# Expert stage: spill and read-back transfers of late chunks issued by ACT, transposes two steps later, three weight loads in flight

## The chip, the cores and the metric

One core of a Trainium2 chip runs the whole program in one launch. The metric is the device time of that launch in microseconds (us). The kernel before has three timed runs with a median of 2337.91 us (2332.89 to 2342.59); one further execution was profiled. The engines are named as in the profile: PE multiplies matrices (PEld is its loading of the stationary operand), DVE and ACT work on vectors, POOL issues indirect DMAs, SP issues the plain loads.

## What is computed

Two transformer blocks on 512 tokens of width 1024, all in float32. The change touches only the last stage, the mixture of experts of the second block. Each token goes to 4 of 32 experts, and each expert is a clamped SwiGLU with its own weights:

```
logits = xt @ router_w + router_b
top_val, top_idx = lax.top_k(logits, TOP_K)          # 4 of 32
gate = softmax(top_val)
# for the tokens of expert e:
gu = xblk @ w_gu[e] + b_gu[e]                         # 1024 -> 2048
g, up = gu[:, :1024], gu[:, 1024:]
g = minimum(g, 7.0); up = clip(up, -7.0, 7.0)
act = (up + 1.0) * (g * sigmoid(1.702 * g))
y = act @ w_down[e] + b_down[e]                       # 1024 -> 1024
out[token] += gate * y
```

An expert's weights are 8 MiB for `w_gu` and 4 MiB for `w_down`. All 32 experts' weights are read once, 384 MiB in all, and the routing decides at run time how many tokens each expert has: 64 on average (512 x 4 / 32).

## The kernel before

Before the experts come the first block, the mixer of the second block and the routing; the experts run from about 984 us of the span to its end, and the last few tens of microseconds add the result to the residual.

**Weights.** `Moe.load` (lines 1625 to 1640) issues one DMA of 1 MiB for each weight tile, on SP's queue: eight `gu` tiles and four `dn` tiles per expert, in the order gu(0), gu(1), dn(0), gu(2), dn(1) and so on. The tiles lie in a ring of 21 slots (`RING = 5, 16`), and a load needs a free slot. `turn` (line 1642) adds a second condition: with `FLIGHT = 2`, a load waits until the load two places before it has landed. Only the first five loads, issued ahead of the stage by `ahead`, are free of it.

**Tokens.** The tokens of an expert are cut in chunks of 64. Chunk 0 is always computed, chunk 1 in two quarter passes of 32 tokens if the expert has over 64 (and over 96) tokens, and each later chunk c if there are over 64c. These are nested `tc.If` blocks on the register `r`. `fetch` gathers a chunk's rows with an indirect DMA on POOL's queue, four transposes on PE bring it into the layout of the stationary operand (`transposed`, tile `ptx`, read out by DVE into `xT` or `turned`), and `up` multiplies with the `gu` tiles and applies the SwiGLU. `down` transposes the activations likewise (read out by ACT), multiplies with the `dn` tiles, scales by the gate on ACT (tile `y`, line 1621) and adds the result to `acc` in DRAM with an indirect DMA on POOL's queue (line 1623).

**Order.** `run` calls, for each e, `tile_up(e)`, the loads that refill the slots it has used, the gathers for later experts, `tile_down(e - 1)` and again the loads that refill its slots. Each queue runs its instructions in order.

**Late chunks.** The activations of chunk 0 and 1 stay on the chip. Those of chunk 2 and later are too many for that: `tile_up` writes the tile `late` (128 x 512, 256 KB) to the DRAM array `spill` (line 1709), and `tile_down` reads it back (lines 1732 and 1747). Both transfers are on POOL's queue. In `down`, `mid` places the four transposes of the next chunk inside the loop over k of 0 to 7, behind the matmuls of k = 4; the last quarter pass, `down(4, e, 1, ...)`, transposes `late` for chunk 2 there.

Of the kernel before, what the change touches and what calls it, by code (L numbers as in the profile page):

```python
# [64 lines left out]
def sm_tile(g, name):  # L65
    return g.ps.tile([P, 512], F32, tag="sm", bufs=2, name=name)


def uid(g, s):
    g.n += 1  # L70
    return f"{s}_{g.n}"
# [47 lines left out]
def behind(g, after, before):  # L119

    g.tc.add_manual_dep(after.ins, before.name, mybir.DependencyInfo(mybir.DependencyClass.NoSync, mybir.DependencyReason.DATA), reason="in turn")
# [1195 lines left out]
NCH = T // CH  # L1317
QUARTERS = 2
RING = 5, 16
FLIGHT = 2  # L1320
LATE = 9
PACE = 2
FILLS = 8
# [3 lines left out]
class Moe:  # L1327
# [265 lines left out]
                mid()  # L1593
        self.swiglu(act, pg, pu, N)

    def down(self, n, e, c, aT, mid=None, after=None):

        g = self.g
        nc = g.nc
        W = self.W["dn", e]  # L1600
        w, N = P // n, D // n
        nb = N // P
        py = sm_tile(g, uid(g, "py"))[:, :N]
        if n == 2:
            d = nc.tensor.matmul(py, self.sel[e], self.bias[:, 2, :], start=True, stop=False)
        else:
            aT = aT[:, c * nb:(c + 1) * nb]
            for odd in range(2):
                x = nc.tensor.matmul(py, self.quarters(e, odd), self.bias[:, 2, odd * N:(odd + 1) * N], start=not odd, stop=False)
                d = d if odd else x  # L1610
        if after is not None:
            behind(g, d, after)
        for k in range(KD):
            lhs = aT[:, k % nb, (k // nb) * w:(k // nb + 1) * w]
            for h in range(n):
                o = (k % 2) * D + h * N
                nc.tensor.matmul(py[h * w:(h + 1) * w, :], lhs, W[k // 2][:, o:o + N], start=False, stop=(k == KD - 1))  # L1617
            if k == 4 and mid is not None:
                mid()
        y = self.pool.tile([P, 512], F32, tag="y", bufs=2, name=uid(g, "y"))[:, :N]  # L1620
        nc.scalar.mul(y, py, self.gate[n][:, c, e:e + 1])
        acc = self.acc if n == 2 else self.acc.rearrange("r (h n) -> (r h) n", h=2)
        nc.gpsimd.indirect_dma_start(out=acc, out_offset=bass.IndirectOffsetOnAxis(ap=self.idx[n][:, c, e:e + 1], axis=0), in_=y, in_offset=None, compute_op=ALU.add)  # L1623
# [18 lines left out]
    def turn(self, d, limit=True):  # L1642

        if limit and len(self.flight) >= FLIGHT:
            self.g.tc.add_manual_dep(d, self.flight[-FLIGHT], mybir.DependencyInfo(mybir.DependencyClass.Sync, mybir.DependencyReason.SCHED_ONLY), reason="few loads at a time")
        self.flight.append(d.name)
# [45 lines left out]
    def tile_up(self, e, xT):  # L1692

        g, tc, r, x = self.g, self.g.tc, self.r[e], self.late
        act0, act1 = self.pool.tile([P, 512], F32, tag="act0", bufs=1, name=uid(g, "act")), self.act1[e % 2]
        more = self.hinted(e, CH, "up")
        self.up(2, e, xT, act0, mid=lambda: self.transposed(self.x1, self.turned(1)))

        def chunk(c, more):
            with tc.If(r > c * CH, label=more):
                then = None
                if c + 1 < NCH:
                    more = self.hinted(e, (c + 1) * CH, "up")
                    self.fetch(x[(c + 1) % 2], e, c + 1)
                    then = lambda: self.transposed(x[(c + 1) % 2], self.turned(c + 1))
                self.up(2, e, self.turned(c), x[c % 2], mid=then, at=6)
                g.nc.gpsimd.dma_start(self.spill[e % 2, c - 2], x[c % 2])
                if c + 1 < NCH:  # L1710
                    chunk(c + 1, more)

        with tc.If(r > CH, label=more):
            with tc.If(r > 2 * CH):
                self.fetch(x[0], e, 2)
            more = self.hinted(e, CH + CH // 2, "up")
            self.up(4, e, self.turned(1), act1[:, 0:256], 0)
            with tc.If(r > CH + CH // 2, label=more):
                more = self.hinted(e, 2 * CH, "up")
                self.up(4, e, self.turned(1), act1[:, 256:512], 1, mid=lambda: self.transposed(x[0], self.turned(2)))  # L1720
                chunk(2, more)
        return act0, act1

    def tile_down(self, e, aT, act1, more, after):
        g, tc, r, a = self.g, self.g.tc, self.r[e], self.late
        self.down(2, e, 0, aT, mid=lambda: self.transposed(act1, self.turned(1), 0.5), after=after)

        def back(c):

            if c < NCH:  # L1730
                with tc.If(r > c * CH):
                    g.nc.gpsimd.dma_start(a[c % 2], self.spill[e % 2, c - 2])

        def chunk(c, more):
            with tc.If(r > c * CH, label=more):  # L1735
                back(c + 2)
                then = None
                if c + 1 < NCH:
                    more = self.hinted(e, (c + 1) * CH, "down")
                    then = lambda: self.transposed(a[(c + 1) % 2], self.turned(c + 1), 0.5)  # L1740
                self.down(2, e, c, self.turned(c), mid=then)
                if c + 1 < NCH:
                    chunk(c + 1, more)

        with tc.If(r > CH, label=more):  # L1745
            with tc.If(r > 2 * CH):
                g.nc.gpsimd.dma_start(a[0], self.spill[e % 2, 0])
                back(3)
            more = self.hinted(e, CH + CH // 2, "down")
            self.down(4, e, 0, self.turned(1))  # L1750
            with tc.If(r > CH + CH // 2, label=more):
                more = self.hinted(e, 2 * CH, "down")
                self.down(4, e, 1, self.turned(1), mid=lambda: self.transposed(a[0], self.turned(2), 0.5))
                chunk(2, more)

    def turned(self, c):
# [191 lines left out]
```

## Time and profile before

| | us |
|---|---|
| median of three runs | 2337.91 |
| range of the runs | 2332.89 to 2342.59 |
| the profiled execution, whole | 2348.3 |
| its span, first to last instruction | 2346.5 |
| PE busy in the span | 2046.9 (87%) |

The profile is of one execution. Its span is 1.8 us shorter than its time, and its time is 10.4 us above the median of the runs. The share of a DMA engine's time that packets took and the rate in GB/s are means over 16 engines. PEclk is TensorE's granted clock as a share of 2.4 GHz, so 0.50 is 1.2 GHz. A row of waits reads: engine and tile, the releaser, us in total, how often, the longest.

### The profile page before, as it was taken

What the parts mean: (1) busy time and instruction counts of PE and PEld (TensorE: products, weight loads), DVE (VectorE), ACT (ScalarE), POOL (GpSimd) and SP (SyncE); (2) the same over time, 40 slices, a digit from 0 to 9 for tenths busy, and PEclk for the clock granted to TensorE, in tenths of its full rate; (3) what the DMA queues carried; (4) which work ended last, traced back from release to release, by engine and by line L of the source; (5) the groups of instructions that cost most, each with busy time, mean ns of one, the idle gap of its engine ahead of it and who ended that gap; (6) DMA issues with size and microseconds to landing.
All of it is one profiled execution on the core that took longest, in us unless ns stands there. A gap on an engine that the chain in (4) does not pass through costs nothing. (4 is left out here: it accounts for less than half of the span.)

```text
span 2346.5 us, 31249 instructions
## 1 busy us (share of the span) xinstructions
PE 2046.9 (87%) x11586; PEld 1116.4 (48%) x11589; DVE 860.5 (37%) x1891; ACT 476.4 (20%) x839; POOL 333.1 (14%) x329
## 2 busy tenths in 40 slices
PE   6999988999998999789898997766798899898763
PEld 6856765688877977533333332221233333333211
DVE  6466659764556556522121121111121122121112
ACT  3345332234434124200100100000000110000001
POOL 2000226310013221100101101000001110101002
PEclk9999999999999999789999999999999999999997
DMA  6451476852237625898939899999996799999986
GB/s 194 119 169 52 154 195 187 252 175 92 98 104 213 213 75 196 345 337 292 327 143 323 300 337 331 356 329 337 325 356 231 257 329 330 336 349 342 333 323 204
DMA packets 213970, 584.24 MB, mean 249 GB/s; under 512 B 32287, under 2 KB 107438, under 8 KB 179822
## 3 DMA queue, kind: packets, MB, share of 16 engines
q1 hardware_dynamic: 182688, 523.74, 62.3%
q0 software_dynamic: 16784, 46.94, 7.4%
q10 hardware_dynamic: 14142, 9.10, 1.3%
q8 instruction: 189, 3.10, 0.5%
q14 instruction: 167, 1.37, 0.2%
HBM read 537.88 MB, written 41.84 MB: 247 GB/s over the span
## 5 line engine op out<-in xcount | busy, mean ns | idle before, releaser
L1587 PE MATMUL pg<-wgu,xT 128*64 128x512 f32 x1024 | 281.5, 620 | 77.9 <-DMA wgu<-in_exp_w_gu 72.5
L1587 PE MATMUL pu<-wgu,xT 128*64 128x512 f32 x1024 | 272.5, 603 | 3.5 <-issue 3.5
L1617 PE MATMUL py<-wdn,aT 128*64 128x512 f32 x1024 | 241.7, 604 | 34.0 <-DMA wdn<-in_exp_w_down 33.9
L1547 DVE TENSOR_TENSOR turned<-ptx,cols 128x512 f32<-128x512 f32 x42 | 29.1, 692 | 461.7 <-PE ptx L1539 460.4
L1561 ACT ACTIVATE th<-gm 128x512 f32<-128x512 f32 (+1 forms) x54 | 30.2, 560 | 777.4 <-DVE gm L1560 762.9
L89 DVE TENSOR_TENSOR wlo<-wst,whi 128x1024 fp32r<-128x1024 f32 (+1 forms) x109 | 135.4, 1242 | 126.6 <-ACT whi L88 126.5
L88 ACT CAST whi<-wst 128x1024 fp32r<-128x1024 f32 (+2 forms) x121 | 123.9, 1027 | 257.7 <-DMA wst<-in_w_ff_in 82.5
L1587 PEld LDWEIGHTS pg<-wgu,xT 128*64 128x64 f32 x1024 | 66.7, 139 | 228.5 <-DMA wgu<-in_exp_w_gu 124.5
L1587 PEld LDWEIGHTS pu<-wgu,xT 128*64 128x64 f32 x1024 | 76.6, 140 | 155.1 <-issue 155.1
L1623 POOL DMA_INDIRECT acc<-y,idx x54 | 85.7, 1587 | 445.5 <-ACTq L1745 226.0
L1617 PEld LDWEIGHTS py<-wdn,aT 128*64 128x64 f32 x1024 | 66.2, 136 | 166.4 <-issue 105.8
L1657 DVE CAST sel<-pick 128x128 fp32r<-128x128 f32 x32 | 7.7, 239 | 357.5 <-PEq L1735 151.1
L1591 PE MATMUL pgu<-wgu,turned 128*32 128x512 f32 x1152 | 128.6, 594 | 0.0
L98 PE MATMUL pf<-hTh,whi 128*128 128x512 f32 (+1 forms) x288 | 111.2, 390 | 8.6 <-ACT whi L88 6.2
L100 PE MATMUL pf<-hTh,wlo 128*128 128x512 f32 (+1 forms) x288 | 109.5, 383 | 6.9 <-DVE wlo L89 6.9
L99 PE MATMUL pf<-hTl,whi 128*128 128x512 f32 (+1 forms) x288 | 109.5, 381 | 0.0
L1531 POOL DMA_INDIRECT xg<-hn,idx x32 | 33.1, 1033 | 491.8 <-PE ptx L1539 415.5
L1617 PE MATMUL py<-wdn,turned 128*32 128x256 f32 (+1 forms) x1280 | 101.2, 418 | 0.0
L98 PE MATMUL plt<-whi,ahi 128*128 128x512 f32 x256 | 99.6, 389 | 0.0
L99 PE MATMUL plt<-wlo,ahi 128*128 128x512 f32 x256 | 99.6, 389 | 0.0
L100 PE MATMUL plt<-whi,alo 128*128 128x512 f32 x256 | 99.1, 389 | 0.0
L1560 DVE TENSOR_SCALAR gm<-pg 128x512 f32<-128x512 f32 x36 | 24.9, 691 | 155.0 <-PE pg L1587 150.4
(541 smaller groups left out, 3423.8 us busy)
## 6 DMA issues: line engine op xcount, KB each, us to landing
wgu<-in_exp_w_gu SPq DMA_DIRECT2D x256, 1024.0 KB
wdn<-in_exp_w_down SPq DMA_DIRECT2D x128, 1024.0 KB
wst<-in_w_in SPq DMA_DIRECT2D x36, 512.0 KB
wst<-in_w_ff_in SPq DMA_DIRECT2D x32, 512.0 KB
wst<-in_w_ff_out SPq DMA_DIRECT2D x32, 512.0 KB
ada_w<-in_ada_w SPq DMA_DIRECT2D x24, 512.0 KB
a<-in_ada_w SPq DMA_DIRECT2D x24, 512.0 KB
wst<-in_w_out SPq DMA_DIRECT2D x16, 512.0 KB
```

Source lines behind the costliest of these rows:

```text
L88: g.nc.scalar.copy(hi, st)
L89: eng.tensor_tensor(out=lo, in0=st, in1=hi.bitcast(F32), op=ALU.subtract)
L98: g.nc.tensor.matmul(out, ah, bh, start=start, stop=False)
L99: g.nc.tensor.matmul(out, ah, bl, start=False, stop=False)
L100: g.nc.tensor.matmul(out, al, bh, start=False, stop=stop)
L1531: self.g.nc.gpsimd.indirect_dma_start(out=x, out_offset=None, in_=self.hn, in_offset=bass.IndirectOffsetOnAxis(ap=self.idx[2][:, c, e:e + ...
L1547: g.nc.vector.tensor_tensor(out=out, in0=src, in1=col(1), op=ALU.mult)
L1561: nc.scalar.activation(th, gm, AF.Tanh, scale=0.851)
L1587: nc.tensor.matmul(ps[h * w:(h + 1) * w, :], lhs, W[k][:, o + h * N:o + (h + 1) * N], start=False, stop=(k == KD - 1))
L1591: nc.tensor.matmul(both[h * w:(h + 1) * w], lhs, wk[:, h], start=False, stop=(k == KD - 1))
L1617: nc.tensor.matmul(py[h * w:(h + 1) * w, :], lhs, W[k // 2][:, o:o + N], start=False, stop=(k == KD - 1))
L1623: nc.gpsimd.indirect_dma_start(out=acc, out_offset=bass.IndirectOffsetOnAxis(ap=self.idx[n][:, c, e:e + 1], axis=0), in_=y, in_offset=None ...
```

## The change

The transfers of late chunks, out to `spill` and back, are issued by ACT (`nc.scalar`) in place of POOL (`nc.gpsimd`). `down` gets an argument `at`, and the calls for quarter pass 1 and for late chunks place the transposes behind k = 6 in place of k = 4; chunk 0 and quarter pass 0 are left as they were. `FLIGHT` is 3: a load waits for the load three places before it.

```diff
--- before.py
+++ after.py
@@ -1317,7 +1317,7 @@
 NCH = T // CH
 QUARTERS = 2
 RING = 5, 16
-FLIGHT = 2
+FLIGHT = 3
 LATE = 9
 PACE = 2
 FILLS = 8
@@ -1593,7 +1593,7 @@
                 mid()
         self.swiglu(act, pg, pu, N)
 
-    def down(self, n, e, c, aT, mid=None, after=None):
+    def down(self, n, e, c, aT, mid=None, after=None, at=4):
 
         g = self.g
         nc = g.nc
@@ -1615,7 +1615,7 @@
             for h in range(n):
                 o = (k % 2) * D + h * N
                 nc.tensor.matmul(py[h * w:(h + 1) * w, :], lhs, W[k // 2][:, o:o + N], start=False, stop=(k == KD - 1))
-            if k == 4 and mid is not None:
+            if k == at and mid is not None:
                 mid()
         y = self.pool.tile([P, 512], F32, tag="y", bufs=2, name=uid(g, "y"))[:, :N]
         nc.scalar.mul(y, py, self.gate[n][:, c, e:e + 1])
@@ -1706,7 +1706,7 @@
                     self.fetch(x[(c + 1) % 2], e, c + 1)
                     then = lambda: self.transposed(x[(c + 1) % 2], self.turned(c + 1))
                 self.up(2, e, self.turned(c), x[c % 2], mid=then, at=6)
-                g.nc.gpsimd.dma_start(self.spill[e % 2, c - 2], x[c % 2])
+                g.nc.scalar.dma_start(self.spill[e % 2, c - 2], x[c % 2])
                 if c + 1 < NCH:
                     chunk(c + 1, more)
 
@@ -1729,7 +1729,7 @@
 
             if c < NCH:
                 with tc.If(r > c * CH):
-                    g.nc.gpsimd.dma_start(a[c % 2], self.spill[e % 2, c - 2])
+                    g.nc.scalar.dma_start(a[c % 2], self.spill[e % 2, c - 2])
 
         def chunk(c, more):
             with tc.If(r > c * CH, label=more):
@@ -1738,19 +1738,19 @@
                 if c + 1 < NCH:
                     more = self.hinted(e, (c + 1) * CH, "down")
                     then = lambda: self.transposed(a[(c + 1) % 2], self.turned(c + 1), 0.5)
-                self.down(2, e, c, self.turned(c), mid=then)
+                self.down(2, e, c, self.turned(c), mid=then, at=6)
                 if c + 1 < NCH:
                     chunk(c + 1, more)
 
         with tc.If(r > CH, label=more):
             with tc.If(r > 2 * CH):
-                g.nc.gpsimd.dma_start(a[0], self.spill[e % 2, 0])
+                g.nc.scalar.dma_start(a[0], self.spill[e % 2, 0])
                 back(3)
             more = self.hinted(e, CH + CH // 2, "down")
             self.down(4, e, 0, self.turned(1))
             with tc.If(r > CH + CH // 2, label=more):
                 more = self.hinted(e, 2 * CH, "down")
-                self.down(4, e, 1, self.turned(1), mid=lambda: self.transposed(a[0], self.turned(2), 0.5))
+                self.down(4, e, 1, self.turned(1), mid=lambda: self.transposed(a[0], self.turned(2), 0.5), at=6)
                 chunk(2, more)
 
     def turned(self, c):
```

## Rows read from the trace of the kernel before

**Rows 1.** The page, busy time: engine, us, share, instructions.
```profile
PE 2046.9 (87%) x11586; PEld 1116.4 (48%) x11589; DVE 860.5 (37%) x1891; ACT 476.4 (20%) x839; POOL 333.1 (14%) x329
```

**Rows 2.** Windows: stretch, length, busy PE/PEld/DVE/ACT/POOL, PEclk, DMA share, GB/s.
```profile
1335.00:1658.00 323.00, 246.15 (x1166) 79.45 (x1163) 54.75 (x94) 23.51 (x38) 27.23 (x21) 0.98 0.93 337
1880.00:2150.00 270.00, 254.88 (x1626) 94.12 (x1624) 55.18 (x102) 26.02 (x45) 33.57 (x25) 0.99 0.95 342
2150.00:2302.00 152.00, 112.08 (x517) 34.41 (x515) 23.35 (x40) 11.07 (x18) 9.37 (x7) 0.98 0.91 328
```

**Rows 3.** Waits of PE from 1335 to 1724 us.
```profile
PE pg L1587 <- DMA wgu<-in_exp_w_gu: 46.5, 35, 4.7
PE py L1617 <- DMA wdn<-in_exp_w_down: 24.5, 20, 2.3
```

**Rows 4.** Waits of PE from 2150 to 2310 us.
```profile
PE pg L1587 <- DMA wgu<-in_exp_w_gu: 26.0, 22, 3.7
PE py L1617 <- DMA wdn<-in_exp_w_down: 9.5, 8, 1.9
```

**Rows 5.** Waits of PE over the expert stage, 984 to 2320 us, transposes alone.
```profile
PE ptx L1539 <- DMA late<-spill: 14.2, 2, 7.5
...
PE ptx L1539 <- issue: 5.3, 1, 5.3
```

**Rows 6.** Waits of SP's queue from 1335 to 1658 us, longest group.
```profile
SPq L1635 <- DMA wgu<-in_exp_w_gu: 139.6, 49, 6.2
```

**Rows 7.** Waits of SP's queue from 1880 to 2302 us, the one for PE.
```profile
SPq L1638 <- PEq L1718: 12.4, 1, 12.4
```

**Rows 8.** DMA view, 1335 to 1658 us: queues (packets, MB, share) and issues.
```profile
q1 hardware_dynamic: 18168, 102.54, 85.2%
q0 software_dynamic: 2320, 5.38, 6.9%
...
wgu<-in_exp_w_gu SPq DMA_DIRECT2D x66, 1024.0 KB
wdn<-in_exp_w_down SPq DMA_DIRECT2D x32, 1024.0 KB
```

**Rows 9.** Timeline of SP's queue, 914 to 919 us: start, us, line, issues.
```profile
914.51 3.48 SPq L1635 DMA_DIRECT2D wgu<-in_exp_w_gu  x5
```

**Rows 10.** Windows, columns as in Rows 2, two more stretches.
```profile
919.00:929.00 10.00, 10.00 (x58) 8.02 (x57) 4.98 (x13) 4.06 (x12) 1.30 (x1) 1.00 0.99 415
1100.00:1150.00 50.00, 44.51 (x333) 16.73 (x329) 7.57 (x15) 4.48 (x8) 6.82 (x5) 0.97 0.99 357
```

**Rows 11.** Timeline, first expert with late chunks, back transfer: start, us, instruction, [idle before].
```profile
1272.09 0.69 ACT L1621 ACTIVATE y<-py,gate 128x512 f32<-128x512 f32 x1 [2.19 <-PE py L1617]
...
1274.04 1.26 POOL L1732 DMA_DIRECT2D late<-spill  x1
...
1276.38 2.37 PE L1617 MATMUL py<-wdn,turned 128*32 128x256 f32 x40
...
1285.45 1.09 PE L1539 MATMUL ptx<-ident,late 128*128 128x128 f32 x4 [6.70 <-DMA late<-spill]
1286.47 2.79 PE L1617 MATMUL py<-wdn,turned 128*32 128x256 f32 x24
```

**Rows 12.** Windows, columns as in Rows 2, just behind that wait.
```profile
1286.00:1290.00 4.00, 4.00 (x30) 1.51 (x30) 0.00 (x0) 1.07 (x2) 0.00 (x0) 0.50 0.94 294
```

**Rows 13.** Timeline, second and third expert with a late chunk.
```profile
1779.90 0.69 ACT L1621 ACTIVATE y<-py,gate 128x512 f32<-128x512 f32 x1 [2.19 <-PE py L1617]
...
1784.69 0.61 POOL L1747 DMA_DIRECT2D late<-spill  x1
...
1832.44 0.69 ACT L1621 ACTIVATE y<-py,gate 128x512 f32<-128x512 f32 x1 [2.19 <-PE py L1617]
...
1835.84 0.60 POOL L1747 DMA_DIRECT2D late<-spill  x1 [0.82 <-DMA xg<-hn,idx]
```

**Rows 14.** DMA view of the whole span, issues of POOL: count, KB, median us to landing.
```profile
spill<-late POOLq DMA_DIRECT2D x4, 256.0 KB, 6.2
late<-spill POOLq DMA_DIRECT2D x4, 256.0 KB, 9.3
...
acc<-y,idx POOLq DMA_INDIRECT x54, 7.6
```

## The prediction, made before the change was run

> **What bounds the kernel now.** I read the page first: PE is busy 87% of the span [rows 1], so a gain must come from the places where PE waits. The waits of PE name two causes that this change touches. The first is weights. From 1335 to 1724 us PE waits 46.5 + 24.5 = 71.0 us for `wgu` and `wdn` tiles [rows 3], and from 2150 to 2310 us another 26.0 + 9.5 = 35.5 us [rows 4]. The windows agree: PE is busy 246 of 323 us in the first stretch and 112 of 152 us at the end, while the DMA engines are at 0.93 and 0.91; between them, from 1880 to 2150 us, PE is busy 255 of 270 us and is the bound itself [rows 2]. The second cause is the read-back of late activations: 14.2 us in two waits, and a third of 5.3 us that the profile files under "issue" [rows 5] and that is the same place in the third expert with a late chunk. In SP's own waits the loads of the first stretch wait for earlier loads, not for PE: the largest group alone is 139.6 us [rows 6]. So a load there is held back by the limit of two in flight, and not by a full ring. From 1880 us on only one wait for PE remains, at the beginning [rows 7].
>
> **Three in flight.** In the first stretch 66 + 32 = 98 loads are issued in 323 us [rows 8], 3.30 us each. How short could that be? Nothing in the trace shows three in flight, so I bound it from both sides.
> The far bound is the five loads that are issued without a limit in 3.48 us [rows 9]: while they land the engines are at 0.99 and move 415 GB/s [rows 10]. 1 MiB at 415 GB/s takes 1.049/0.415 = 2.53 us. POOL's traffic takes 6.9% of the engines in the first stretch [rows 8], 0.069 x 323 / 98 = 0.23 us per load, and stays. That is 2.76 us, or 0.54 us saved per load.
> The near bound is the idle share alone: the engines idle 7% [rows 2], and if packets keep their present length a full queue gives 3.30 x 0.93 = 3.07 us, 0.23 us saved. Packets are longer now than in the stretch of five loads: weights take 0.852 x 323 / 98 = 2.81 us of engine time per load against 0.99 x 2.53 = 2.50. If that is restarting after gaps, it goes too; if it is interference, it stays.
> Below both lies nothing: if one of the 16 engines is always the last, a load more in flight only lets the other 15 wait longer. A loss per load is excluded as far as I see, since the queue works its loads in the order in which they were issued.
> I take 3.00 us, 0.30 saved, near the bound of the idle share, since three is nearer to two than to five.
> First stretch: 98 x 0.30 = 29 us, under the 71.0 that PE waits. The first expert's loads start from a full ring and can't be early, so I count 25 (19 for 0.23, 46 for 0.54).
> Last stretch: loads that come earlier between 1880 and 2150 us fill the ring while PE is the bound and shorten nothing at once. What counts is the loads of the five experts that are computed at the end, 60 x 0.30 = 18 us, under the cap of 35.5 (14 for 0.23, 32 for 0.54).
>
> **Read-back by ACT, transposes at k = 6.** In the first expert with late chunks ACT's `y` ends at 1272.09 + 0.69 = 1272.78. POOL issues its scatter first and the read-back at 1274.04; PE reaches the transposes at 1276.38 + 2.37 = 1278.75 and starts them at 1285.45, 6.70 us late [rows 11]. ACT has no scatter ahead of it. I give it 0.4 us for the branch, so 0.8 us are won in the issue. In the second and third expert ACT's `y` ends at 1780.59 and 1833.13, POOL's issue is at 1784.69 and 1835.84 [rows 13], so 3.7 and 2.3 us are won. `at=6` puts 16 more matmuls ahead of the transposes, 16 x 2.37/40 = 0.95 us of work per wait.
> How long the transfer takes on ACT's queue no row shows. On POOL's queue the read-back lands after 9.3 us in the median, and the write-out, as large but mostly with no scatter queued just ahead, after 6.2 [rows 14]. With the latency unchanged 0.8 + 3.7 + 2.3 + 3 x 0.95 = 9.7 us of the 19.5 go. With 6.2 us the first lands at 1279.4, when PE has work until 1279.7, and nearly all go.
> The waits have a second price. Behind the first one the four transposes take 1.09 us and 24 matmuls 2.79 us, where 40 took 2.37 [rows 11], so 24 should take 1.42; the granted clock there is 0.50, the level of 1.2 GHz, and PE was idle just before [rows 12]. That is 1.4 us on the matmuls and some 0.5 on the transposes, 1.9 per wait, 5.7 for three, and it goes if the wait gets short. So this part is worth 9.7 to 25 us. I take 21, near the upper end, because the row of the write-out is the nearer one: it too is a plain transfer with nothing of its own queue ahead.
> All of it is on the path: in those experts PE, not the loads, is late, and the loads behind them wait for its slots, up to the last wait for PE at 1880 us [rows 7].
> A page speaks against it. The Trainium skill's page "DMA: Bandwidth & Descriptors", section "Issuing engines are not separate DMA queues", says that DMAs of all issuing engines run on the same 16 engines and interleave, so that another issuer only saves the time to start them. By that this part gives the lower end, 9.7 us.
> The rest costs about nothing. The write-out is behind ACT's tanh and has to wait for DVE's last operations, but the next ACT instruction of that block waits for PE anyway, and it happens four times [rows 14]. POOL loses eight issues. Later transposes leave eight matmuls of cover for ACT's read-out, 0.5 us against the 0.69 of an ACT operation on such a tile [rows 11]: at most 0.2 us in some ten passes, cover being the next pass's bias matmuls.
>
> **Sum.** 25 + 18 + 21 = 64 us. The profiled execution took 2348.3 us, so it would take 2284.3; it stood 10.4 us above the median of the runs, 2337.9, which gives 2274.
>
> **The rivals.**
> (a) Packets were long only because of restarts, and three in flight act like five: 46 + 32 + 21 = 99, 2239 us. For it: 415 GB/s at 0.99 [rows 10]. Against it: POOL had nothing to move then.
> (b) There is a ceiling below that. In the expert stage the best stretch of 50 us that I found moved 357 GB/s at 0.99 of the engines [rows 10]. At that rate a load takes 3.30 x 337/357 = 3.12 us, 0.18 saved: 16 + 11 + 21 = 48, 2290 us. The Trainium skill's page "DMA: Bandwidth & Descriptors", section "Where 436 GB/s comes from", holds that for transfers from HBM a limit of some 358 GB/s per core binds; the row of 415 GB/s disagrees with it, so I give this less than the forecast.
> (c) One engine is always the last: flight gives nothing, the read-back 21, 2317 us.
> (d) SP's loads begin to wait for ACT's conditional transfers, since both are then of the hardware kind, while POOL's are software [rows 8]. A transfer of 6.2 to 9.3 us ahead of the loads, at the two places where a stretch of loads begins, costs up to 18: 2292 us.
> (e) Slower. With the engines never idle, POOL's accumulating scatters take longer. They go one behind the other, 7.6 us each in the median, 54 of them [rows 14]. An expert with quarter passes makes three or more in some 16 us of PE work, so PE begins to wait for the `y` tiles when one takes clearly over 7.6 us. With half as much again, 3.8 us more for some 24 scatters behind the first two of an expert, 91 us are lost against the 64 won, 27 more than before: 2365 us. Against it: PE waits for no scatter by name now, and POOL's share is 6.9%.
>
> **How the numbers follow.** Chances: forecast 0.46, (a) 0.14, (b) 0.18, (c) 0.12, (d) 0.05, (e) 0.05. Leaving out (e) and the outer half of (a) and of (c), whose read-back may give only 9.7 and end at 2328, gives a range of 2242 to 2322. A measurement of this kernel can tell about 0.5% from no change, 11.7 us: faster means under 2326. That is all but (e) and a part of (c): faster 0.89, same 0.06, slower 0.05.
>
> **What would show it.** Right: in the first stretch 98 loads take some 294 us, the DMA share is 0.97 or more, PE's waits for weights fall from 106 us to about 60, and the waits for `late<-spill` are under 2 us each at a clock of 1.00. Wrong: the share rises and the rate stays (interference, b), the loads keep 3.30 us (c), SP waits for ACT (d), or new waits of PE or ACT for `acc` transfers (e). If `late` lands 9 us after ACT's issue, the queue was not what made it slow.

## The result, and the profile after

The changed kernel takes 2282.44 us in the median (2280.64 to 2284.60) against 2337.91: a ratio of 0.975 [0.972, 0.979]. In a second measurement it took 2277.12 against 2341.29, 0.972 [0.968, 0.976]. The prediction was 2274, with a range of 2242 to 2322. The profiled execution took 2280.64 us, with a span of 2278.8.

The page, busy time, in the columns of [rows 1]:

```profile
PE 2042.2 (90%) x11586; PEld 1126.5 (49%) x11589; DVE 860.2 (38%) x1891; ACT 476.3 (21%) x839; POOL 327.8 (14%) x321
```

Windows, in the columns of [rows 2]. The first one begins where the first of [rows 2] does:

```profile
1335.00:1600.00 265.00, 236.53 (x1141) 82.66 (x1137) 54.03 (x92) 21.63 (x35) 25.53 (x20) 0.97 1.02 400
1880.00:2150.00 270.00, 236.39 (x1465) 87.53 (x1463) 51.83 (x94) 23.25 (x40) 28.17 (x21) 0.95 0.89 343
2150.00:2260.00 110.00, 92.03 (x503) 32.40 (x498) 18.53 (x32) 12.01 (x23) 11.22 (x9) 0.94 0.88 322
```

The first stretch has changed as hoped: 400 GB/s in place of 337, and PE busy for 89% of it in place of 76%. The queue of the weight loads there, in the columns of [rows 8]:

```profile
q1 hardware_dynamic: 17750, 99.66, 92.9%
```

The second one has got worse. PE was busy for 255 of 270 us there before [rows 2], and now for 236. The stretch holds later experts now, since the changed kernel is ahead; but counted by matmuls, the same work that took 270 us there before takes 298 us now, from 1831 to 2129 us. So something new holds PE, and the waits of PE from 980 us to the end name it:

```profile
PE ptx L1539 <- PEq L1745: 25.5, 20, 3.9
PE ptx L1539 <- PEq L1751: 14.2, 5, 4.9
PE ptx L1539 <- PEq L1713: 12.4, 20, 4.7
PE ptx L1539 <- DMA wgu<-in_exp_w_gu: 12.0, 1, 12.0
PE ptx L1539 <- SPq L1746: 10.1, 2, 8.2
PE ptx L1539 <- issue: 9.5, 1, 9.5
PE ptx L1539 <- DMA late<-spill: 9.0, 3, 3.8
PE ptx L1539 <- PEq L1735: 8.8, 5, 6.1
PE pg L1587 <- DMA wgu<-in_exp_w_gu: 5.6, 6, 1.5
PE ptx L1539 <- PEq L1702: 5.0, 6, 1.6
...
PE ptx L1539 <- PEq L1718: 3.3, 5, 0.7
...
PE py L1617 <- DMA wdn<-in_exp_w_down: 1.7, 3, 0.9
```

The waits for weights, 106 us in [rows 3] and [rows 4], are 5.6 + 1.7 = 7.3 us. The read-back has fallen from 19.5 us [rows 5] to 9.0. In their place stand two other things: long branches, and SP. The rows with "PEq" are PE waiting for its own sequencer at a branch. The same rows of the kernel before, which the prediction did not use, add up to 49.2 us:

```profile
PE ptx L1539 <- PEq L1745: 13.5, 20, 2.5
PE ptx L1539 <- PEq L1751: 10.2, 5, 4.1
PE ptx L1539 <- PEq L1735: 10.1, 6, 3.6
PE ptx L1539 <- PEq L1713: 8.2, 20, 0.6
PE ptx L1539 <- PEq L1702: 3.9, 6, 0.7
PE ptx L1539 <- PEq L1718: 3.3, 5, 0.7
```

After the change they are 69.2 us. The 9.5 us under "issue" belong to them, since two branches of 5.9 and 5.1 us stand ahead of that transpose: 78.7 us. In the sequencer's records there were 25 branch instructions of over 0.5 us, 67 us in all; now there are 36, 129 us in all. (Each is counted 0.1 us shorter than its record, here and in all that follows; the records themselves add up to 69.5 and 132.2 us.)

The DMA packets of the trace show what such a branch waits for. The DMA view of the whole span has this line, the same before and after the change (189 packets of 16 KB):

```profile
q8 instruction: 189, 3.10, 0.5%
```

Each of the 25 long branches of the kernel before ends 1.2 to 1.5 us behind the end of one of these packets, and each of the 36 of the changed kernel 1.3 to 1.6 us behind. So a long branch is PE's code arriving late. The packet itself takes as long as before (1.0 and 1.1 us in the mean); it starts later, 0.34 us behind the start of the branch in the mean before and 1.17 us after.

The second new thing is PE waiting for SP. In expert 17 (counted from 0, as in the code; the expectations call it the seventeenth) the transposes of `late` wait 11.96 us, because POOL's gather into `late` was issued only at 1643.65 (timeline: start, us, engine, line, instruction, idle before and what ended it):

```profile
1634.34 4.50 PE L1591 MATMUL pgu<-wgu,turned 128*32 128x512 f32 x40
...
1643.65 0.96 POOL L1531 DMA_INDIRECT late<-hn,idx  x1 [21.59 <-DMA wgu<-in_exp_w_gu]
...
1650.80 1.08 PE L1539 MATMUL ptx<-ident,late 128*128 128x128 f32 x4 [11.96 <-DMA wgu<-in_exp_w_gu]
```

The row says "wgu", but no weight is needed there. The instruction records of the two queues show what POOL waited for (start us, queue, line, instruction):

```
1621.64  POOL  L1531  record of its wait for count 102
1640.26  SP    L1635  issues a wgu load
1640.64  SP    L1745  branch: block not taken
1641.05  SP    L1745  adds to count 100
1641.14  SP    L1745  adds to count 102
1641.21  SP    L1745  adds to count 103
1641.26  POOL  L1531  record of its wait for counts 103 and 100
```

POOL's next record comes 0.05 us behind SP's count on 103. A transfer that ACT issues is counted on the same semaphores as SP's weight loads: the four read-backs on 103, 105 and 109, which have 35 to 60 weight loads each in the expert stage. Where its conditional block is not taken, something must add the counts that the transfer would have added, and in this program that is SP, at its own copy of the branch. SP takes its instructions in order, and ahead of that branch it stood in its limited loads. So POOL stood too, and behind POOL, PE. The other wait of this kind is in the down part of expert 25, where PE needs the read-back tile although that expert has no late chunk:

```profile
2071.78 3.23 PE L1617 MATMUL py<-wdn,turned 128*32 128x256 f32 x56
...
2083.17 1.09 PE L1539 MATMUL ptx<-ident,late 128*128 128x128 f32 x4 [8.17 <-SPq L1746]
```

In the records SP passes its branch of line 1746 at 2082.77 and has added the counts by 2083.04; PE's record of its wait for one of them, 109, follows at 2083.07. In the kernel before, SP passes the same branches and adds nothing.

### The profile page after: what moved, and what is told of

Read it like the earlier page. It is cut to its first block, busy times and chain, and to the rows that moved or that the text cites. A ratio compares the mean times of both kernels' runs of the same rounds, so it can differ in the third digit from the quotient of the medians.

```text
span 2278.8 us, 31675 instructions
## 1 busy us (share of the span) xinstructions
PE 2042.2 (90%) x11586; PEld 1126.5 (49%) x11589; DVE 860.2 (38%) x1891; ACT 476.3 (21%) x839; POOL 327.8 (14%) x321
## 5 line engine op out<-in xcount | busy, mean ns | idle before, releaser
L1617 PE MATMUL py<-wdn,aT 128*64 128x512 f32 x1024 | 237.1, 603 | 2.2 <-DMA wdn<-in_exp_w_down 1.7
L1617 PEld LDWEIGHTS py<-wdn,aT 128*64 128x64 f32 x1024 | 68.8, 138 | 128.2 <-issue 122.3
L1539 PE MATMUL ptx<-ident,act 128*128 128x128 f32 x256 | 43.9, 296 | 60.1 <-PEq L1745 25.5
```

The costliest lines, as they stand in the source:

```text
L1539: d = g.nc.tensor.transpose(pt[:, b * P:(b + 1) * P], x[:, b * P:(b + 1) * P], g.ident)
```

## The experiments

One theory and its rivals: **the third load** takes away nearly all waits for weights and makes PE's branches longer; **the read-back on ACT's queue** ties POOL and PE to SP, and loses what it wins. A rival puts all new waits down to ACT's transfers. The table adds up PE's waits from 980 us on, in us. "Branches" are the transposes that wait for "PEq", and a long "issue" wait at `act` behind branches. "SP" are waits that end with SP's counts; up to 1.8 us of them are weight loads that landed 0.03 us ahead of such a count. Waits that end with the landing of a read-back are under "late", whatever the view names. The last column is the sum of PE's branch instructions over 0.5 us and their number. Ratios are to the kernel before as measured beside each kernel (medians of 2341 to 2347 us in the later measurements).

| kernel | median us | ratio | weights | late | branches | SP | long branches |
|---|---|---|---|---|---|---|---|
| before | 2337.91 | 1 | 106.4 | 19.5 | 49.2 | 0 | 67 (25) |
| act_only_f2 | 2327.68 | 0.994 [0.991, 0.997] | 98.2 | 7.9 | 54.3 | 0 | 83 (28) |
| f3_only | 2265.10 | 0.967 [0.963, 0.970] | 9.6 | 25.9 | 68.8 | 0 | 112 (33) |
| f3_late_pool | 2261.67 | 0.967 [0.963, 0.971] | 11.1 | 22.8 | 69.3 | 0 | 118 (34) |
| f4_only | 2258.86 | 0.965 [0.961, 0.968] | 5.5 | 25.9 | 74.7 | 0 | 121 (33) |
| f5_late_pool | 2262.91 | 0.966 [0.962, 0.969] | 13.0 | 23.2 | 69.7 | 0 | 120 (34) |
| after_again | 2277.12 | 0.972 [0.968, 0.976] | 6.0 | 8.7 | 84.3 | 24.8 | 138 (35) |
| f3_back_act | 2279.59 | 0.974 [0.970, 0.977] | 7.6 | 13.3 | 75.8 | 23.5 | 125 (35) |
| f3_spill_act | 2262.24 | 0.966 [0.962, 0.969] | 13.6 | 20.5 | 65.2 | 1.5 | 121 (35) |
| half_pool | 2189.65 | 0.934 [0.931, 0.937] | 0 | 12.4 | 47.5 | 0 | 78 (28) |
| half_act | 2188.19 | 0.932 [0.929, 0.935] | 0 | 2.7 | 53.3 | 0 | 90 (29) |
| f4_early_back | 2242.34 | 0.956 [0.954, 0.958] | 15.2 | 9.3 | 64.4 | 0 | 89 (34) |
| f2_early_back | 2338.01 | 0.996 [0.994, 0.999] | 88.1 | 3.9 | 60.0 | 0 | 73 (27) |

### The two parts alone, and a fourth load

**f3_only**, the kernel before with

```diff
-FLIGHT = 2
+FLIGHT = 3
```

> The kernel before with three loads in flight and nothing else. Theory 1 (two prices): the third load removes nearly all of PE's waits for weights (106 us before, 7 after the whole change), and makes PE's slow branches longer, because the fetch of the code behind them shares the DMA engines with three loads: the branches over 0.5 us, 67 us in all before and 129 after, are 110 to 140 us here, and no wait of PE or POOL for SP's queue or for `wgu` ahead of `late` is there. Time 2260 to 2275, below the 2282 of the whole change. Theory 2 (the transfers on ACT's queue are the whole price): the long branches and the waits for SP both come from ACT's transfers in the conditional blocks; the branches stay near 67 us and the time is about 2338 - 99 = 2240.

Measured: 2265.10 us, 0.967. Theory 1 holds and theory 2 falls: with no transfer on ACT's queue PE waits 68.8 us at branches in place of 49.2 (among them 28.4 in place of 13.5 at line 1745). The longest groups that are not weights, and the weights themselves:

```profile
PE ptx L1539 <- PEq L1745: 28.4, 20, 3.9
PE ptx L1539 <- DMA late<-spill: 19.1, 2, 10.4
PE ptx L1539 <- PEq L1735: 13.3, 6, 4.6
...
PE py L1617 <- DMA wdn<-in_exp_w_down: 4.9, 8, 0.8
PE pg L1587 <- DMA wgu<-in_exp_w_gu: 4.7, 6, 1.4
```

**act_only_f2**, the whole change with

```diff
-FLIGHT = 3
+FLIGHT = 2
```

> The whole change without its third load: transfers of late chunks on ACT's queue, transposes behind k = 6, two loads in flight. Theory 1: branches stay near 67 us; PE waits for the read-back about 9 to 10 us in place of 19.5; a wait of POOL for loads ahead of the gather into `late` and waits of PE for SP's queue are there as in the whole change (22 us), part of it hidden since loads are late anyway: 2330 to 2350, no gain. Theory 2: branches at 110 to 130 us too, 2350 to 2370. By the prediction's third term it would have been 2338 - 21 = 2317.

Measured: 0.994 [0.991, 0.997], some 14 us gained where theory 1 gave none. The waits for the read-back fall from 19.5 to 7.9 us, a little below the 9 to 10 of theory 1. (The view puts 3.9 of the 7.9 down to SP, but these two waits end as the read-backs of 1784.41 and 1828.99 land, 8.8 and 8.3 us after their issue.) The waits for weights are 8.2 us shorter and those for branches 5.1 us longer, so the three make 14.7. No wait of PE for SP is there, since PE is late for weights at those places anyway. POOL still waits: in expert 17 its gather into `late` is freed only as SP passes line 1745 at 1675.0 us, but PE stands for a weight load of that expert until 1682.6. Two loads in flight hide the price.

**f3_late_pool**, the whole change with the three transfers back on POOL's queue:

```diff
-g.nc.scalar.dma_start(a[0], self.spill[e % 2, 0])
+g.nc.gpsimd.dma_start(a[0], self.spill[e % 2, 0])
```

and likewise the read-back of later chunks and the write-out.

> The whole change with the transfers of late chunks back on POOL's queue: three in flight, transposes behind k = 6. Theory 1: the waits for SP and the 12 us wait for the gather into `late` are gone, the waits for the read-back are 12 to 17 us, the branches stay at 110 to 140 us: 2258 to 2272, 10 to 20 us below the whole change. Theory 2: branches near 67 us, 2235 to 2245. If ACT's queue is worth what the prediction gave it, this kernel is slower than the whole change.

Measured: 2261.67 us, as expected by theory 1, and some 15 us below the whole change, though the waits for the read-back, 22.8 us, are above the 12 to 17 expected. It doesn't differ from f3_only by more than the measurement tells, so the later transposes alone are worth 0 to 3 us (waits for the read-back 22.8 in place of 25.9).

**f4_only**, the kernel before with `FLIGHT = 4`.

> The kernel before with four loads in flight: a dose for the branches. Theory 1: waits for weights stay near nothing, the slow branches get longer again (over 130 us, the longest 7 us or more), the time is 2262 to 2285, no better than with three. Theory 2: branches near 67 us, time within 5 us of three in flight alone.

Measured: 2258.86 us; the branches 121 us, not over 130, and the time below the 2262 to 2285 of theory 1. So a fourth load brings little, and the branches don't grow with each load. The loads of the first stretch agree: the 98 loads of [rows 8] come every 3.31 us with two in flight, 2.78 with three and 2.79 with four.

### Which transfer ties PE to SP

**after_again** is the changed kernel itself, measured beside the next three.

> The whole change once more, on the chip of the next kernels: 2276 to 2290 us, some 17 us above three in flight alone (2265); PE's waits for weights under 10 us, its slow branches 120 to 140 us, 10 us or more of waits for SP's queue, and the late gather of the seventeenth expert held until SP has passed a branch.

Measured: 2277.12 us. The two waits are at the same places, 12.1 us in expert 17 and 9.0 us in expert 25.

**f3_back_act**, the whole change with

```diff
-g.nc.scalar.dma_start(self.spill[e % 2, c - 2], x[c % 2])
+g.nc.gpsimd.dma_start(self.spill[e % 2, c - 2], x[c % 2])
```

> The whole change with the write-out back on POOL's queue; the read-back stays on ACT's. Theory 1 (the read-back is what couples: the tile `late` then waits for the counts that SP adds when a block is not taken): PE's waits for SP and POOL's late gather are as in the whole change, 2272 to 2286. Theory 2 (the write-out couples): both gone, 2252 to 2264.

**f3_spill_act**, the whole change with the two read-backs on `g.nc.gpsimd` and the write-out left on ACT.

> The whole change with the read-back on POOL's queue; the write-out stays on ACT's. Theory 1: PE's waits for SP's queue are gone, the gather into `late` has to wait only where an earlier write-out stands, 2258 to 2270, close to three in flight alone. Theory 2: as the whole change, 2272 to 2286.

Measured: 2279.59 and 2262.24 us. Theory 1 holds: the read-back makes PE wait, the write-out doesn't. (SP adds counts for the write-out too, at its branch of line 1713, but nobody stands for long for them.) One row of each kernel tells it, the transposes of `late` (busy us, mean ns, then idle before them and what ended it). With the read-back on ACT:

```profile
L1539 PE MATMUL ptx<-ident,late 128*128 128x128 f32 x80 | 14.8, 314 | 36.7 <-DMA wgu<-in_exp_w_gu 18.5 <-DMA late<-hn,idx 12.5 <-DMA late<-spill 3.5
```

With the write-out on ACT:

```profile
L1539 PE MATMUL ptx<-ident,late 128*128 128x128 f32 x80 | 14.4, 308 | 20.5 <-DMA late<-spill 14.1 <-issue 6.4
```

In the first, the 12.5 us stand in expert 17 and 8.8 of the 18.5 in expert 25; the other 9.7 end as read-backs land. The gather of expert 17 stands 21.5 us on POOL in the first, 1.8 us in the second.

**f5_late_pool** is f3_late_pool with `FLIGHT = 5`.

> Five loads in flight, transfers of late chunks on POOL's queue, transposes behind k = 6. If more loads in flight make code fetches longer in proportion, the slow branches are over 130 us and the time is above the 2259 of four in flight; if the DMA engines are full from three on, the branches stay at 115 to 125 us and the time is 2250 to 2260.

Measured: 2262.91 us, branches 120 us. From three on, neither the branches nor the time depend on the number in flight. The time lies 3 us above the 2250 to 2260 expected.

### Half the traffic

Both kernels leave out the second half of every weight tile and multiply the first one twice:

```diff
-d = g.nc.sync.dma_start(w, g.a["exp_w_gu_2"][0, e, k * P:(k + 1) * P, :])
+d = g.nc.sync.dma_start(w[:, :D], g.a["exp_w_gu_2"][0, e, k * P:(k + 1) * P, :D])
...
-for o, ps in ((0, pg), (D, pu)):
+for o, ps in ((0, pg), (0, pu)):
```

and the same in the quarter passes and in `down`. **half_pool** has the transfers on POOL's queue.

> Three in flight, transfers of late chunks on POOL's queue, transposes behind k = 6, as before in this series, but each weight load brings 512 KB in place of 1 MiB: the second half of every weight tile is left out and the first half is multiplied twice, so PE's work is the same and the experts' traffic is half. Theory 1 (a slow branch of PE is code that waits behind weight packets): the branches over 0.5 us fall from 118 us to 20 to 45, below the 67 of the kernel before though PE is never late for weights, and the time is 2190 to 2225. Theory 2 (branches are slow because PE comes to them earlier, before its code): they stay at 105 to 125 us, and the time is 2245 to 2255.

**half_act** has them on ACT's.

> The whole change with the same half loads (the second half of every weight tile is left out, the first is multiplied twice). Theory 1 (the price of the read-back on ACT's queue is that SP, which has to add the counts of a block that is not taken, is held at its loads): SP now comes to its branches early, the waits of PE for SP and of POOL's late gather are under 3 us, and the time lies between 12 us below half loads with POOL's transfers and 3 us above. Theory 2 (the added semaphore work itself is the price): 10 to 18 us above.

Measured: 2189.65 and 2188.19 us. First the tie to SP. With half loads SP is no longer held in its loads, and no wait of PE for SP is left although the read-back is on ACT's queue. The row of the transposes of `late`, half loads with the transfers on ACT's queue:

```profile
L1539 PE MATMUL ptx<-ident,late 128*128 128x128 f32 x80 | 13.0, 285 | 2.9 <-DMA late<-spill 2.7
```

The same row with the transfers on POOL's queue, where only the read-back itself is waited for:

```profile
L1539 PE MATMUL ptx<-ident,late 128*128 128x128 f32 x80 | 14.0, 300 | 12.4 <-DMA late<-spill 8.6 <-issue 3.8
```

So the added counts cost nothing by themselves; it is SP's coming late to them that costs. Here theory 1 is shown.

The branches are less clear. They fall from 118 to 78 us, and PE's waits for them from 69.3 to 47.5 us, about the level of two full loads in flight. Most of what the third load added goes with the traffic, although PE never waits for weights there. But 78 us are above the 45 that theory 1 allowed, so traffic alone doesn't explain them. Code is late in these too: each of the 28 ends 1.3 to 1.5 us behind a packet of q8. In the mean the packet starts 0.51 us behind the branch, against 1.07 in f3_late_pool and 0.34 in the kernel before.

### The read-back ahead of the scatter

**f4_early_back** is f4_only with the later transposes, and the conditional read-back moved ahead of chunk 0's pass:

```diff
+        with tc.If(r > 2 * CH):
+            g.nc.gpsimd.dma_start(a[0], self.spill[e % 2, 0])
+            back(3)
         self.down(2, e, 0, aT, mid=..., after=after)
...
-            with tc.If(r > 2 * CH):
-                g.nc.gpsimd.dma_start(a[0], self.spill[e % 2, 0])
-                back(3)
```

> Four in flight, transfers on POOL's queue, transposes behind k = 6, and the conditional read-back of chunk 2 is issued ahead of `down` of chunk 0 in place of behind it, so ahead of that pass's scatter, about 6 to 10 us earlier. If the read-back's place in the queue is what makes it late, the waits for `late` fall from 17 to 19 us to under 5 and the time is 2240 to 2252; if the transfer itself is slower then, since it falls among more loads, the waits stay over 10 and the time is 2253 to 2263.

Measured: 2242.34 us, 0.956: the fastest here that does all the work, 35 to 40 us below the whole change. In the DMA view from 980 us on (issues, KB each, median us to landing) the read-back of f4_early_back lands 7.0 us after its issue:

```profile
late<-spill POOLq DMA_DIRECT2D x4, 256.0 KB, 7.0
```

The same view of f3_late_pool, where the read-back is behind the scatter (in f4_only, with four loads in flight as here, 11.1):

```profile
late<-spill POOLq DMA_DIRECT2D x4, 256.0 KB, 10.6
```

The waits for `late` fall to 9.3 us, not under 5. The first expert with late chunks no longer waits for the read-back, the other two still wait 4.1 and 5.2 us. The branches are shorter too, 89 us against 121, with full loads.

**f2_early_back** is the same with `FLIGHT = 2`.

> The kernel before with two loads in flight, transfers on POOL's queue, transposes behind k = 6, and the read-back of chunk 2 issued ahead of `down` of chunk 0. If the read-back's price is its place behind the scatters on POOL's queue, the transfer lands after about 7 us as it does with four in flight, the waits for `late` fall from 19.5 to under 10 us and the time is 2322 to 2336 against 2342 to 2347 for the kernel before. If the shorter branches with the early read-back and four in flight (89 us against 121) come from the place of the added block, the branches are below 67 us here too, 40 to 60; if they came from chance, they are 60 to 85.

Measured: 0.996 [0.994, 0.999], so 3 to 15 us gained; waits for `late` 3.9 us, branches 73 us. The median of 2338.01 is 2 us above the range expected, but the waits for the read-back are as short as they should be with two loads as well. The added block doesn't shorten branches there (73 against 67), so why they are shorter with four in flight stays open.

## Why the prediction was right, and by which errors

The forecast was 64 us below, and 56 came (64 in the second measurement). It is near because two terms were off in opposite directions, which is luck.

- **What bounds the kernel** [rows 2 to 4]: right. Weights and the read-back were the two waits to win, and 99 of the 106 us for weights are gone.
- **Three in flight**: the mechanism was right, the size too small. The step that failed is "I take 3.00 us, 0.30 saved". Loads come every 2.78 us, 0.53 saved, at the far bound of 0.54. Packets did get shorter, as the case of restarts supposed: the weight queue took 92.9% of the engines' time over 265 us for 96 loads, 0.929 x 265 / 96 = 2.56 us per load, against 2.81 before [rows 8]. The two terms, 25 + 18 = 43, were worth 3.3% of 2347, 78 us, in f3_only. That is just the 46 + 32 of rival (a).
- **Why 97 us less waiting for weights gave 78**: in f3_only the waits for branches took back 20 us and those for the read-back 6 (it lands later among more loads), while PE's own work ran 8 us shorter (1140.7 before, 1132.7 here, from 980 us on). 97 - 20 - 6 + 8 = 79, of the 83 us between the two profiled executions. No term of the prediction had PE's branches.
- **The ceiling of rival (b)**: fallen. 400 GB/s were moved for 265 us, where the best stretch before had 357 [rows 10]. The Trainium skill's page "DMA: Bandwidth & Descriptors", section "Where 436 GB/s comes from", puts a limit of some 358 GB/s on what one core moves from HBM; here the measurement stands against it. Three to five loads in flight don't go beyond, though: 400 and 402 GB/s with three and four.
- **Rival (c)**, one engine always last, has fallen with the same rows.
- **Read-back by ACT**: 21 us were expected. Alone with two loads in flight it gave 14. With three, where it was to be used, it cost 12 to 20 (f3_only and f3_late_pool against the whole change, by the ratios). Two steps failed. The first is the landing: "With 6.2 us the first lands at 1279.4". On ACT's queue the four read-backs took 7.2, 9.4, 8.2 and 9.4 us by the records of their semaphores; POOL's scatter is issued within a microsecond of each. The Trainium skill's page "DMA: Bandwidth & Descriptors", section "Issuing engines are not separate DMA queues", had said as much, and the trace agrees: with two loads in flight the waits fell by 11.6 us, near the lower end of 9.7 that the prediction gave by that page. The 6.2 us of the write-out was the row of a transfer with no scatter beside it, and f4_early_back shows that the place in the order, not the engine, was worth it with four loads in flight. The step also took one transfer for two. In the first expert with late chunks PE is let go only as the second read-back lands, that of chunk 3, at 1286.17; the first had landed at 1283.07. In the kernel before it is the same, 1285.11 and 1283.65. The clock went as supposed in part: two of the three late waits are followed by transposes of 0.70 and 0.63 us in place of 1.09.
- The second failed step is **"The rest costs about nothing"**. Rival (d) had the right pair, SP's loads and ACT's conditional transfers, at 18 us and a chance of 0.05, but the wrong direction. SP doesn't wait for the transfers; POOL and PE wait for SP, 23 us. Set against f3_late_pool, the trace of the whole change has these 23.2 us, 9.4 more at branches, 13.8 less for the read-back, 3.8 less for weights and 4.4 more of PE's own work: 19.4 of the 19.6 us between the two spans. With the read-back on ACT's queue the branches are longer in each pair, by 5 to 15 us (54.3 and 49.2, 78.7 or 84.3 and 69.3, 53.3 and 47.5); why is not shown.
- **Rival (e)**: the scatters did become slower, 9.3 us in the median against 7.6 [rows 14], and PE waits for none of them. Its price never came due.
- **What would show it**: the DMA share passed (1.02 against 0.97 or more), the loads were faster than said (98 x 2.78 = 272 us against 294), the waits for weights fell to 7, not 60, and the waits for `late` were 2.5 to 3.8 us, not under 2.

What stays open: why the code packets of long branches start when they do, and with it why half loads leave 78 us of them, and why the early read-back shortens them with four loads and not with two. That a long branch is code arriving late is shown by the packets; that weight packets hold the code back fits the fall with half the traffic, but is not shown.

## What to carry to other kernels

Before you move a conditional transfer to another engine, look whose semaphores count it: if they are shared with a long queue of limited loads, a block that is not taken can make everybody wait for that queue. To get a transfer in sooner, move it ahead of what it stands behind, rather than to another queue: with four loads in flight that won some 20 us here, while the other queue with three cost 12 to 20. With two in flight both win, 3 to 15 and 7 to 20 us, and can't be told apart. And when one wait is taken away, price the next one in the list, the branches of the sequencer among them; here they took back 20 of the 97 us that the third load had won.

## What the hardware showed that was not expected

- Two 1 MiB loads in flight kept the DMA engines at 0.93 and 337 GB/s; three gave 400 GB/s, and four or five no more.
- PE's branches are not free beside traffic: 25 long ones with 67 us at two loads in flight, 34 with 118 us at three, 28 with 78 us at three half loads. Each of these ends 1.2 to 1.5 us behind a 16 KB packet of the instruction queue, for two and three loads and half loads alike.
- A 256 KB read-back takes 7.0 us ahead of a scatter and 11.1 behind it on the same queue, both with four loads in flight, and 7.2 to 9.4 on another queue beside it, with three.
